# Weight blocks with their columns from the last to the first, streamed with a step of minus one

## The chip, the cores and the metric

The kernel runs on one core of one Trainium2 chip. The metric is the device time of one execution in microseconds, as the median of several runs. A hardware profile of one execution goes with it.

## What is computed

One decoder layer over 256 tokens of width 4096. The input is normed, multiplied with one wide weight, split into the operands of two token mixers, and each mixer's result is projected, gated, added, and projected once more:

```
h = rms_norm(x, norm_gains)
z = h @ w_in                       # gq gk gv gg gdec sq sk sv sg ga gb
o_a = rms_norm(gla_mix(gq, gk, gv, log_a(gdec)), gla_norm_gains)
y_a = (o_a * silu(gg)) @ w_gla_out
o_b = swa_sink_mix(sq, sk, sv, sinks)
y_b = (o_b * silu(sg)) @ w_swa_out
merged = sigmoid(ga + b_gates[0]) * y_a + sigmoid(gb + b_gates[1]) * y_b
out = rms_norm(x + merged @ w_out, final_norm_gain)
```

All of it is in float32.

## The kernel before

Nearly all of the work is in `gemm` (line 125). One call computes 512 columns of a product of all 256 tokens with one weight. The tokens are two tiles of 128; each has an accumulator of 128x512 numbers in PSUM. The depth of the product (4096, or 2048 for w_gla and w_swa) is cut into k tiles of 128, and two k tiles make a chunk.

For every chunk SyncE issues one load of 512 KB into a `raw` tile (line 148; four buffers). ScalarE casts it to float32r, a float32 with fewer mantissa bits, which gives `hi` (line 154; three buffers), and VectorE puts what is left, raw - hi, into `lo` (line 155; three buffers). Load and split carry a higher priority than the rest, so that they run ahead of the products (line 147). The left operand `lhs` has been split in the same way. `products` (lines 131 to 138) then issues, for one token tile and each of the chunk's k tiles, three products: left hi with hi, left hi with lo, left lo with hi. Of each, the token tile's 128x128 block is the stationary operand, and the 512 columns of hi or lo are the moving operand. A chunk thus feeds 2 k tiles x 3 products x 2 token tiles = 12 products.

The blocks of w_in come in the order of `BLOCKS`: query, key, value and gate of the linear attention, key and value of the window attention, then w_gla's eight blocks, the query and gate blocks of the window attention, and for each of eight blocks of the merge gate A, gate B and w_swa. The eight blocks of w_out stand last. In the last one, chunks near the end are kept in a tile `hold` until the second token tile's products use them (`trail`). The first block is preceded chunk by chunk by the load and split of the input (`first_inputs`).

Small products of the attentions and transposes, on float32 data, lie between the blocks. The low-rank decay (lines 208 to 216) has a weight `wdec` of its own, which is loaded and split apart from `gemm`; its product at line 215 has 32 columns of `wd` as the stationary operand and the 512 columns of one k tile of `hT` as the moving one.

On the host, `_tiles` (line 566) puts each weight into the order in which its chunks are loaded: [block, K group, partition, k tile, 512]. `wdec` does not go through it.

Of the kernel before, what the change touches and what calls it, by code (L numbers as in the profile page):

```python
# [28 lines left out]
STG = 3  # L29
NEG = -3.4028234663852886e38  # L30

# 512-column blocks of w_in, in the order in which the host lays them out.
BLOCKS = []
for _g in range(2):
    BLOCKS += [("gq", _g), ("gk", _g)]
# [11 lines left out]
def trunk_kernel(  # L47
# [18 lines left out]
    nc = tc.nc  # L66
# [18 lines left out]
    nc.gpsimd.memset(mhalf, -0.5)  # L85

    def rms_scale(o, ssum, n):
        """o = (ssum / n + eps) ** -0.5"""
        nc.vector.tensor_scalar(o, ssum, 1.0 / n, EPS, ALU.mult, ALU.add)
        nc.gpsimd.tensor_tensor(o, o, mhalf[:, : o.shape[1]], ALU.pow)  # L90

# [1 line left out]
    hT = big.tile([P, KT, 2, S], F32R, tag="hT", name="hT")  # L93

    xsb = big.tile([P, KT, S], F32, tag="oT", name="xsb")

    def first_inputs(gp, ssq):
        """Loads the input as the first block needs it; its squares add up in ssq."""

        def before(k0, n):  # L100
            with tc.high_priority(PRIO):
                if k0 < 4 or k0 % 4 == 0:
                    m = n if k0 < 4 else 4
                    nc.sync.dma_start(xsb[:, k0 : k0 + m, :], xT[:, k0 : k0 + m, :])
                for kt in range(k0, k0 + n):
                    g = gin_sb[:, kt : kt + 1]
                    nc.scalar.activation(hT[:, kt, 0, :], xsb[:, kt, :], AF.Copy, scale=g)
                    nc.vector.scalar_tensor_tensor(
                        hT[:, kt, 1, :], xsb[:, kt, :], g, hT[:, kt, 0, :].bitcast(F32), ALU.mult, ALU.subtract
                    )  # L110
            xr = xsb[:, k0 : k0 + n, :]
            if k0 < KW:
                nc.scalar.activation(ssq[:, k0 : k0 + n, :], xr, AF.Square)
                return
            sq = gp.tile([P, KW, S], F32, tag="sq", name=f"sq{k0}", bufs=2)
            nc.scalar.activation(sq, xr, AF.Square)
            nc.gpsimd.tensor_tensor(ssq, ssq, sq, ALU.add)

        return before
# [3 lines left out]
    RAMP = [(k, 1) for k in range(KW)] + WHOLE[1:]  # L123

    def gemm(name, lhs, w, nkt, before=None, chunks=WHOLE, trail=0, hold=None):
        """Both token tiles of lhs.T @ w for one block of 512 columns. The second tile's products
        with the last `trail` chunks come after all of the first tile's; those of these chunks
        that the staging area can't keep until then are in `hold`."""
        acc = [acc_ps.tile([P, NB], F32, tag="acc", name=f"{name}_a{t}") for t in range(NT)]

        def products(t, k0, n, hi, lo):
            ts = slice(t * P, (t + 1) * P)
            for i in range(n):
                kt = k0 + i
                lh, ll = lhs[:, kt, 0, ts], lhs[:, kt, 1, ts]
                nc.tensor.matmul(acc[t], lh, hi[:, i, :], start=kt == 0, stop=False)  # L136
                nc.tensor.matmul(acc[t], lh, lo[:, i, :], start=False, stop=False)  # L137
                nc.tensor.matmul(acc[t], ll, hi[:, i, :], start=False, stop=kt == nkt - 1)  # L138

        chunks = [c for c in chunks if c[0] < nkt]  # L140
        held = []
        for ci, (k0, n) in enumerate(chunks):
            left = len(chunks) - ci
            if before is not None:
                before(k0, n)
            with tc.high_priority(PRIO):
                raw = stage.tile([P, n, NB], F32, tag="raw", name=f"{name}_r{k0}", bufs=4)
                nc.sync.dma_start(raw, w[k0 // KW][:, k0 % KW : k0 % KW + n, :])
                if STG < left <= trail:
                    hi, lo = hold[:, trail - left, 0], hold[:, trail - left, 1]  # L150
                else:
                    hi = stage.tile([P, n, NB], F32R, tag="hi", name=f"{name}_h{k0}")
                    lo = stage.tile([P, n, NB], F32R, tag="lo", name=f"{name}_l{k0}")
                nc.scalar.copy(hi, raw)  # L154
                nc.vector.tensor_tensor(lo, raw, hi.bitcast(F32), ALU.subtract)  # L155
            products(0, k0, n, hi, lo)
            if left <= trail:
                held.append((k0, n, hi, lo))
            else:
                products(1, k0, n, hi, lo)  # L160
        for h in held:
            products(1, *h)
        return acc
# [5 lines left out]
        return rstd[:, t : t + 1]  # L169

    def split_to(dst, src_ps):
        """dst[:, ..hi/lo.., :] from a PSUM tile of the same layout less the hi/lo axis."""
        hi, lo = dst
        nc.scalar.copy(hi, src_ps)
        nc.vector.tensor_tensor(lo, src_ps, hi.bitcast(F32), ALU.subtract)

    def transpose_split(oT, kt0, src, nk, name):
        """src [tokens, t, nk*128] -> oT[:, kt0:kt0+nk, hi/lo, tokens]"""
        for k2 in range(0, nk, 2):
            tp = pst(f"{name}_t{k2}")  # L180
            for k in range(2):
                for t in range(NT):
                    c = (k2 + k) * P
                    nc.tensor.transpose(
                        tp[:, k * S + t * P : k * S + (t + 1) * P], src[:, t, c : c + P], ident
                    )
            v = tp.rearrange("p (k s) -> p k s", k=2)
            ks = slice(kt0 + k2, kt0 + k2 + 2)
            split_to((oT[:, ks, 0, :], oT[:, ks, 1, :]), v)

    # ================= gated linear attention =================
    with tc.tile_pool(name="gla", bufs=1) as gp:
        ssq = gp.tile([P, KW, S], F32, name="ssq")
        q0 = zblock("gq", 0, before=first_inputs(gp, ssq), chunks=RAMP)
        k0 = zblock("gk", 0)
        oaT = big.tile([P, OKT, 2, S], F32R, tag="oT", name="oaT")

        # per-token scale of the input norm
        xps = pst("xps")
        for t in range(NT):  # L200
            for i in range(KW):
# [2 lines left out]
                )  # L204
        rms_scale(rstd, xps[:, 0:NT], DM)

        # low-rank decay input, transposed: rows 0-15 from w's high part, 16-31 from its low part
        wd_raw = stage.tile([P, KT, RANK], F32, tag="raw", name="wd_raw", bufs=4)
        nc.sync.dma_start(wd_raw, wdec)
        wd = gp.tile([P, KT, 2, RANK], F32R, name="wd")  # L210
# [26 lines left out]
        nc.gpsimd.memset(cmask.rearrange("p (n c) -> p n c", c=CH)[:, :, 0:1], 0.0)  # L237

        def headsT(name, acc, scale):
            """[tokens, 4 heads x 128] in PSUM -> [128, head, token]"""  # L240
            zt = gp.tile([P, NT, NB], F32, tag="zt", name=f"{name}_z")
            for t in range(NT):
                nc.scalar.activation(zt[:, t, :], acc[t], AF.Copy, scale=rs(t))
            o = gp.tile([P, 4, S], F32, tag=name[:2], name=f"{name}T")
            for j2 in range(2):
                tp = pst(f"{name}_tp{j2}")
                for j in range(2):
                    for t in range(NT):
                        c = (j2 * 2 + j) * P
                        nc.tensor.transpose(  # L250
                            tp[:, j * S + t * P : j * S + (t + 1) * P], zt[:, t, c : c + P], ident
                        )
                nc.vector.tensor_scalar(
                    o[:, 2 * j2 : 2 * j2 + 2, :].rearrange("p h s -> p (h s)"), tp, scale, None, ALU.mult
                )
            return o
# [4 lines left out]
        for g in range(2):  # L261
            accq = q0 if g == 0 else zblock("gq", g)
            qT = headsT(f"gq{g}", accq, DK**-0.5)

            # log decays of the group's heads and their running sums in each chunk
            l = gp.tile([P, 4, S], F32, tag="e0", name=f"l{g}")
            for j2 in range(2):
                lp = pst(f"lp{g}{j2}")
# [10 lines left out]
            a = gp.tile([P, 4, S], F32, tag="e1", name=f"a{g}")  # L279
# [34 lines left out]
            )  # L314
            nc.scalar.activation(d, d, AF.Exp)
            nc.vector.tensor_tensor(kT, kT, d, ALU.mult)
            # keys of chunks 0 and 1 as chunks 2 and 3 see them
            k2 = gp.tile([P, 4, 2 * CH], F32, tag="k2", name=f"k2{g}")
            k3 = gp.tile([P, 4, 2 * CH], F32, tag="k3", name=f"k3{g}")
            nc.vector.tensor_tensor(  # L320
# [5 lines left out]
            for p in range(2):  # L326
                pi = 2 * g + p
                accv = zblock("gv", pi)
                v = gp.tile([P, NT, 2 * DV], F32, tag="v", name=f"v{pi}")
                for t in range(NT):  # L330
                    nc.scalar.activation(v[:, t, :], accv[t], AF.Copy, scale=rs(t))

                # o = A @ v, a head at a time; A is kept transposed, [key, query]
                accg = None
                oraw = gp.tile([P, 2, NT, DV], F32, tag="oraw", name=f"oraw{pi}")
                ss = gp.tile([P, 2 * NT], F32, tag="ss", name=f"ss{pi}")
# [51 lines left out]
                        nc.vector.tensor_tensor(gt4[:, t, j, :], ov, gt4[:, t, j, :], ALU.mult)  # L388
                transpose_split(oaT, pi * 4, gt, 4, f"oa{pi}")

    # ================= sliding-window attention =================
    late = ctx.enter_context(tc.tile_pool(name="late", bufs=1))
    ya = late.tile([P, NT, DM], F32, tag="ya", name="ya")
    with tc.tile_pool(name="swa", bufs=1) as sp:
# [100 lines left out]
                nc.vector.tensor_tensor(on[:, t, :], on[:, t, :], sg, ALU.mult)  # L495
            transpose_split(obT, i * 4, on, 4, f"ob{i}")

    # ================= gates and merge =================
    def merged(n):
        transpose_split(mT, n * 4, ya[:, :, n * NB : (n + 1) * NB], 4, f"m{n}")  # L500

# [21 lines left out]
                nc.vector.tensor_tensor(sig[1][:, t, :], acc[t], sig[1][:, t, :], ALU.mult)  # L523
                nc.vector.tensor_tensor(ya[:, t, cs], ya[:, t, cs], sig[1][:, t, :], ALU.add)

    # ================= output projection, residual, final norm =================
    with tc.tile_pool(name="fin", bufs=1) as fp:
        gf = fp.tile([P, DM], F32, name="gf")
        nc.scalar.dma_start(gf, gfin.partition_broadcast(P))
        hold = None  # L530
# [33 lines left out]


def _tiles(w, nblk):
    """[K, nblk*512] -> [block, K group, partition, k tile, 512], contiguous for each load."""
    import numpy as np

    k = w.shape[0]  # L570
    w = w.reshape(k // (KW * P), KW, P, nblk, NB)
    return np.ascontiguousarray(w.transpose(3, 0, 2, 1, 4))


# [53 lines left out]
```

## Time and profile before

| | us |
|---|---|
| median of 3 runs | 2496.63 |
| lowest and highest | 2496.22, 2498.13 |
| span of the profiled execution, first to last instruction | 2494.7 |
| TensorE shows matmuls | 2469.9 |
| TensorE shows weight loads (beside the matmuls) | 2033.3 |
| VectorE busy | 1306.1 |
| ScalarE busy | 1093.1 |
| GpSimd busy | 41.4 |
| HBM read and written | 468.23 MB, 4.19 MB |

In a row of the profile PE is TensorE's matmul, PEld its load of a stationary operand, DVE is VectorE, ACT ScalarE, POOL GpSimd and SP SyncE; SPq is SyncE's queue. L136 is line 136 of the kernel. A matmul is shown from its start to a modelled end, and the following ones start before that end, so its duration is longer than its place in the stream. A product on float32 operands shows as two records, one on float32r operands as one.

### The profile page before, as it was taken

How to read it: one execution, taken by the hardware profiler on the slowest of the kernel's cores; microseconds unless marked ns; L12 is line 12 of the kernel's file. 1: busy time of each engine (PE TensorE's matmuls, PEld its weight loads, DVE VectorE, ACT ScalarE, POOL GpSimd, SP SyncE). 2: the span in 40 equal slices, each digit the busy share in tenths (PEclk: the TensorE clock that was granted, in tenths of full speed). 3: DMA queues.
4: the chain of work that ended last, by engine and by line, in shares of the span. 5: the costliest groups of instructions: out<-in, count | busy, mean ns of one | idle time of the engine just before them, and what ended most of it. 6: DMA issues, size and time to landing. Idle time of an engine off the chain costs nothing.

```text
span 2494.7 us, 28744 instructions
## 1 busy us (share of the span) xinstructions
PE 2469.9 (99%) x11220; PEld 2033.3 (82%) x11220; DVE 1306.1 (52%) x1303; ACT 1093.1 (44%) x1289; POOL 41.4 (2%) x52
## 2 busy tenths in 40 slices
PE   8999999999999999999999999999999999999998
PEld 6788888888888888888888888888888888888886
DVE  8565555545444455555555454555545456544544
ACT  6444444434444444544444444444444444444443
POOL 4000000000000000000000000000000000000000
PEclk9999999999999999999999999999999999999999
DMA  7455555445555545454465556665666555665655
GB/s 258 156 175 188 170 175 195 175 168 188 194 192 195 193 148 193 150 171 166 150 211 199 198 198 197 197 202 197 198 196 198 194 194 177 236 211 203 211 203 186
DMA packets 132985, 474.32 MB, mean 190 GB/s; under 512 B 15056, under 2 KB 15440, under 8 KB 132720
## 3 DMA queue, kind: packets, MB, share of 16 engines
q1 hardware_dynamic: 127584, 461.69, 54.5%
q10 hardware_dynamic: 5264, 10.79, 1.4%
q8 instruction: 88, 1.44, 0.2%
q14 instruction: 49, 0.40, 0.0%
HBM read 468.23 MB, written 4.19 MB: 189 GB/s over the span
## 4 chain that ended last, share of the span: by engine, by line
PE 95%; DVE 2%; issue 1%; ACT 1%; DMA 0%; POOL 0%; SPq 0%; ACTq 0%; POOLq 0%; DVEq 0%
PE ga_a L137 5%; PE ga_a L136 5%; PE gb_a L137 5%; PE gb_a L136 5%; PE ga_a L138 5%; PE gb_a L138 5%; PE o_a L136 5%; PE o_a L137 5%; PE o_a L138 5%; PE sg_a L137 2%; PE sg_a L136 2%; PE sg_a L138 2%; PE sq_a L138 2%; PE sq_a L137 2%; PE ya_a L136 2%; PE ya_a L137 2%
## 5 line engine op out<-in xcount | busy, mean ns | idle before, releaser
L155 DVE TENSOR_TENSOR ga_l<-ga_r,ga_h 128x1024 fp32r<-128x1024 f32 x128 | 156.8, 1225 | 171.6 <-ACT ga_h L154 171.6
L155 DVE TENSOR_TENSOR gb_l<-gb_r,gb_h 128x1024 fp32r<-128x1024 f32 x128 | 156.9, 1225 | 171.1 <-ACT gb_h L154 171.1
L155 DVE TENSOR_TENSOR o_l<-o_r,o_h 128x1024 fp32r<-128x1024 f32 x124 | 152.0, 1225 | 161.4 <-ACT o_h L154 161.3
L154 ACT CAST ga_h<-ga_r 128x1024 fp32r<-128x1024 f32 x128 | 135.2, 1057 | 209.8 <-PE ga_a L138 171.5
L154 ACT CAST gb_h<-gb_r 128x1024 fp32r<-128x1024 f32 x128 | 135.2, 1056 | 204.5 <-PE gb_a L138 159.4
L154 ACT CAST o_h<-o_r 128x1024 fp32r<-128x1024 f32 x124 | 131.0, 1056 | 193.2 <-PE o_a L138 186.2
L138 PE MATMUL ga_a<-ga_h,hT 128*128 128x512 f32 x512 | 199.4, 389 | 0.0
L137 PE MATMUL ga_a<-ga_l,hT 128*128 128x512 f32 x512 | 199.2, 389 | 0.0
L136 PE MATMUL ga_a<-ga_h,hT 128*128 128x512 f32 x512 | 199.2, 389 | 0.0
L138 PE MATMUL gb_a<-gb_h,hT 128*128 128x512 f32 x512 | 199.2, 389 | 0.0
L136 PE MATMUL gb_a<-gb_h,hT 128*128 128x512 f32 x512 | 199.2, 389 | 0.0
L137 PE MATMUL gb_a<-gb_l,hT 128*128 128x512 f32 x512 | 199.2, 389 | 0.0
L138 PE MATMUL o_a<-o_h,mT 128*128 128x512 f32 x496 | 193.0, 389 | 0.0
L137 PE MATMUL o_a<-o_l,mT 128*128 128x512 f32 x496 | 193.0, 389 | 0.0
L136 PE MATMUL o_a<-o_h,mT 128*128 128x512 f32 x496 | 192.9, 389 | 0.0
L155 DVE TENSOR_TENSOR ya_l<-ya_r,ya_h 128x1024 fp32r<-128x1024 f32 x64 | 78.4, 1226 | 95.6 <-ACT ya_h L154 95.6
L155 DVE TENSOR_TENSOR sq_l<-sq_r,sq_h 128x1024 fp32r<-128x1024 f32 x64 | 78.4, 1225 | 84.8 <-ACT sq_h L154 84.8
L155 DVE TENSOR_TENSOR yb_l<-yb_r,yb_h 128x1024 fp32r<-128x1024 f32 x64 | 78.4, 1225 | 82.8 <-ACT yb_h L154 82.8
L155 DVE TENSOR_TENSOR gg_l<-gg_r,gg_h 128x1024 fp32r<-128x1024 f32 x64 | 78.3, 1224 | 75.9 <-ACT gg_h L154 75.9
L155 DVE TENSOR_TENSOR sg_l<-sg_r,sg_h 128x1024 fp32r<-128x1024 f32 x64 | 78.3, 1223 | 72.7 <-ACT sg_h L154 72.7
L154 ACT CAST sg_h<-sg_r 128x1024 fp32r<-128x1024 f32 x64 | 67.4, 1053 | 111.0 <-PE sg_a L138 94.7
L155 DVE TENSOR_TENSOR gv_l<-gv_r,gv_h 128x1024 fp32r<-128x1024 f32 x64 | 78.2, 1224 | 67.9 <-ACT gv_h L154 67.9
(278 smaller groups left out, 5568.3 us busy)
## 6 DMA issues: line engine op xcount, KB each, us to landing
ga_r<-in_win_dram SPq DMA_DIRECT2D x128, 512.0 KB, 4.3
gb_r<-in_win_dram SPq DMA_DIRECT2D x128, 512.0 KB, 4.2
o_r<-in_wout_dram SPq DMA_DIRECT2D x128, 512.0 KB, 3.3
gv_r<-in_win_dram SPq DMA_DIRECT2D x64, 512.0 KB, 3.2
gg_r<-in_win_dram SPq DMA_DIRECT2D x64, 512.0 KB, 3.3
ya_r<-in_wgla_dram SPq DMA_DIRECT2D x64, 512.0 KB, 3.2
sq_r<-in_win_dram SPq DMA_DIRECT2D x64, 512.0 KB, 3.2
sg_r<-in_win_dram SPq DMA_DIRECT2D x64, 512.0 KB, 3.3
```

The lines of the kernel that those rows point to most:

```text
L136: nc.tensor.matmul(acc[t], lh, hi[:, i, :], start=kt == 0, stop=False)
L137: nc.tensor.matmul(acc[t], lh, lo[:, i, :], start=False, stop=False)
L138: nc.tensor.matmul(acc[t], ll, hi[:, i, :], start=False, stop=kt == nkt - 1)
L154: nc.scalar.copy(hi, raw)
L155: nc.vector.tensor_tensor(lo, raw, hi.bitcast(F32), ALU.subtract)
```

## The change

The columns of each block of 512 are laid out in reverse on the host, and the products read them in reverse:

```diff
--- before.py
+++ after.py
@@ -133,9 +133,9 @@
             for i in range(n):
                 kt = k0 + i
                 lh, ll = lhs[:, kt, 0, ts], lhs[:, kt, 1, ts]
-                nc.tensor.matmul(acc[t], lh, hi[:, i, :], start=kt == 0, stop=False)
-                nc.tensor.matmul(acc[t], lh, lo[:, i, :], start=False, stop=False)
-                nc.tensor.matmul(acc[t], ll, hi[:, i, :], start=False, stop=kt == nkt - 1)
+                nc.tensor.matmul(acc[t], lh, hi[:, i, ::-1], start=kt == 0, stop=False)
+                nc.tensor.matmul(acc[t], lh, lo[:, i, ::-1], start=False, stop=False)
+                nc.tensor.matmul(acc[t], ll, hi[:, i, ::-1], start=False, stop=kt == nkt - 1)
...
@@ -564,12 +564,12 @@
 def _tiles(w, nblk):
...
     k = w.shape[0]
     w = w.reshape(k // (KW * P), KW, P, nblk, NB)
-    return np.ascontiguousarray(w.transpose(3, 0, 2, 1, 4))
+    return np.ascontiguousarray(w[..., ::-1].transpose(3, 0, 2, 1, 4))
```

The four weights w_in, w_gla, w_swa and w_out all go through `_tiles`, and all their products through these three lines. The two reversals cancel, so column j of an accumulator is column j of the block as before. What the diff changes beside this are comments.

## Rows read from the trace of the kernel before

**Rows 1.** The page's head: the span, and each engine's busy time, share and instructions.
```profile
span 2494.7 us, 28744 instructions
PE 2469.9 (99%) x11220; PEld 2033.3 (82%) x11220; DVE 1306.1 (52%) x1303; ACT 1093.1 (44%) x1289; POOL 41.4 (2%) x52
```

**Rows 2.** The page's 40 slices: busy tenths, DMA share in tenths, GB/s.
```profile
PE   8999999999999999999999999999999999999998
...
DMA  7455555445555545454465556665666555665655
GB/s 258 156 175 188 170 175 195 175 168 188 194 192 195 193 148 193 150 171 166 150 211 199 198 198 197 197 202 197 198 196 198 194 194 177 236 211 203 211 203 186
```

**Rows 3.** Stretches, TensorE alone: length, busy (records), granted clock, DMA share, GB/s.
```profile
core 0: us, PE busy (x), PEclk, DMA share, GB/s
0.00:60.00 60.00, 49.07 (x199) 1.00 0.75 262
60.00:2480.00 2420.00, 2416.82 (x11006) 1.00 0.56 188
```

**Rows 4.** The chain that ended last: shares of the span by engine.
```profile
PE 95%; DVE 2%; issue 1%; ACT 1%; DMA 0%; POOL 0%; SPq 0%; ACTq 0%; POOLq 0%; DVEq 0%
```

**Rows 5.** Costliest groups: out<-in, shapes, count, busy us, mean ns, idle before, releaser.
```profile
L155 DVE TENSOR_TENSOR ga_l<-ga_r,ga_h 128x1024 fp32r<-128x1024 f32 x128 | 156.8, 1225 | 171.6 <-ACT ga_h L154 171.6
...
L154 ACT CAST ga_h<-ga_r 128x1024 fp32r<-128x1024 f32 x128 | 135.2, 1057 | 209.8 <-PE ga_a L138 171.5
...
L137 PE MATMUL ga_a<-ga_l,hT 128*128 128x512 f32 x512 | 199.2, 389 | 0.0
L136 PE MATMUL ga_a<-ga_h,hT 128*128 128x512 f32 x512 | 199.2, 389 | 0.0
```

**Rows 6.** Timeline, TensorE, a quiet stretch: start us, length us, instruction; 19 products.
```profile
1899.81 0.39 PE L136 MATMUL yb_a<-yb_h,obT 128*128 128x512 f32 x1
1900.03 0.39 PE L137 MATMUL yb_a<-yb_l,obT 128*128 128x512 f32 x1
1900.26 0.39 PE L138 MATMUL yb_a<-yb_h,obT 128*128 128x512 f32 x1
...
1903.89 0.39 PE L136 MATMUL yb_a<-yb_h,obT 128*128 128x512 f32 x1
```

**Rows 7.** Instructions of a tile: shortest/median/longest ns, first and last start us.
```profile
L136 PEld LDWEIGHTS ga_a<-ga_h,hT x512: 187/188/192, 1256.6 to 2062.1; 128*128 128x128 f32 x171
```

**Rows 8.** The same view of line 215, the low-rank product.
```profile
L215 PEld LDWEIGHTS dps<-hT,wd x32: 107/108/113, 102.8 to 109.8; 128*32 128x32 f32 x32
L215 PE MATMUL dps<-hT,wd x32: 387/392/400, 102.9 to 110.0; 128*32 128x512 f32 x32
```

**Rows 9.** DMA issues: count, KB each, median us from issue to landing.
```profile
ga_r<-in_win_dram SPq DMA_DIRECT2D x128, 512.0 KB, 4.3
```

**Rows 10.** Waits: ScalarE's longest on TensorE, and all of TensorE's; us, times, longest.
```profile
ACT ga_h L154 <- PE ga_a L138: 171.5, 104, 1.7
...
PE gq_a L136 <- ACT gq_h L154: 5.7, 2, 5.4
PE gq_a L137 <- DVE gq_l L155: 5.2, 6, 1.9
PE op L365 <- POOL ats L359: 2.4, 4, 0.6
PE gv_a L137 <- DVE gv_l L155: 0.5, 1, 0.5
PE gk_a L137 <- DVE gk_l L155: 0.3, 1, 0.3
```

**Rows 11.** Timeline, TensorE, products on float32 operands, two records each.
```profile
163.24 0.59 PE L366 MATMUL op<-v,ats 128*128 128x256 f32 x2
163.68 0.59 PE L367 MATMUL op<-v,ats 128*128 128x256 f32 x2
164.11 0.33 PE L345 MATMUL at<-qs,ks 128*128 128x64 f32 x2
```

**Rows 12.** Timeline, TensorE, a block's start: the first and last of nine products.
```profile
115.20 0.39 PE L138 MATMUL gv_a<-gv_h,hT 128*128 128x512 f32 x1
...
117.04 0.39 PE L137 MATMUL gv_a<-gv_l,hT 128*128 128x512 f32 x1
```

## The prediction

> **What bounds the kernel now.** I read the page's head first [rows 1]: TensorE shows work in 2469.9 of 2494.7 us, VectorE in 1306.1, ScalarE in 1093.1. A matmul's end is modelled in this profile, so a busy share near 99% alone doesn't prove that TensorE is the limit. The 40 slices come next [rows 2]: TensorE is at nine tenths in all but the first and the last, and the DMA engines are mostly half to two thirds busy. From 60 to 2480 us the granted clock is 1.00, its upper level of 2.4 GHz [rows 3]. The chain of work that ended last then settles it [rows 4]: 95% of the span is TensorE's own, and no other engine has more than 2%.
>
> What sets TensorE's own time is read from the distance between starts, not from durations. A product of the weight stream (128x512, lines 136 to 138) is shown as 389 ns long [rows 5], but the next one starts long before that. In the timeline of a quiet stretch 19 products start between 1899.81 and 1903.89 us [rows 6]: 4.08 us over 18 steps is 226.7 ns each. There are 38 blocks of w_in with 32 k tiles, 8 blocks each of w_gla and w_swa with 16, and 8 blocks of w_out with 32, each k tile with 3 products for 2 token tiles: (38x32 + 16x16 + 8x32) x 6 = 10368 products, of the 11220 matmul records of [rows 1]. 10368 x 226.7 ns = 2350 us, or 94% of the span, which agrees with the chain. So every nanosecond on the distance of these products is worth 10.4 us, or 0.42%. That is the number on which the whole case hangs.
>
> Does the moving stream (the 512 columns of hi or lo) set the 226.7 ns, or the load of the stationary tile in front of each product? A load takes 188 ns [rows 7], and it starts beside the product before it. The low-rank product (line 215) streams 512 columns of the same type against a stationary tile of only 32 columns: its loads take 108 ns, yet 32 of them start from 102.9 to 110.0 us [rows 8], 7.1/31 = 229 ns apart. A shorter load doesn't bring the products closer, so the load isn't the limit. At 2.4 GHz one column a cycle makes 512/2.4 = 213.3 ns; 13.3 ns of the 226.7 are something else, and no row tells whether the stream itself needs them.
>
> **The change, part by part.**
> The layout: each block's 512 columns are reversed on the host, ahead of the launch. The shape, the bytes and the order of chunks in memory are as before, so a load stays 512 KB from the same places, with 4.3 us to landing [rows 9]; nothing is added to SyncE's queue, and no DMA is moved past another. Cost 0.
> The split: the cast (1057 ns) and the subtraction (1225 ns) run over 128x1024 numbers whose order has no meaning for them [rows 5]. Cost 0. Even a change here would lie in cover: a chunk feeds 12 products, 12 x 226.7 = 2720 ns, and ScalarE waits for TensorE to give a staging buffer back rather than the other way [rows 10].
> The tiles that aren't reversed: the decay weights (lines 208 to 212) aren't laid out by the function that reverses, and their product at line 215 isn't touched. `hold`, in the last block, is filled from reversed chunks and read by the same three lines, so it fits. The results leave each product in the old order, and everything behind the accumulators is as before. Cost 0.
> The products: the moving operand now starts at column 511 and goes down by 4 bytes at a time. Instructions, their count, stationary tiles, outputs and waits are the same. The only unknown of the case is whether TensorE reads a descending row as fast as an ascending one. No row shows a step of minus one on any engine, so I bound it from both sides. Below: at best the 13.3 ns above the 512 columns go away, 10368 x 13.3 = 138 us. Above: the fp32 products at lines 366 and 367 take their moving columns at a lower rate, under the same full clock. Two records of 256 columns start 163.24, two more 163.68, the next group 164.11 us [rows 11], so a record takes 0.87/4 = 217 ns, 0.85 ns a column against 0.44. A descending read at that rate would make 435 ns a product, 10368 x (435 - 226.7) = +2160 us. Between these far ends I take 0: the nearest rows by far are the same products themselves, with the same type, the same number of bytes from the same row of the same tile, read in four-byte steps.
> The page "SBUF — State Buffer" of the Trainium skill, in the section Door 1: The DMA port swizzle (its note on cachelines), bears on this: on-chip memory is read in lines of 16 bytes, accesses that stay in a line run at full rate, and at least two of them are needed to cover a new line. By that rule a descending fp32 row still has four accesses a line, and its cost would be nothing; no run here shows it yet.
>
> The sum: 0 on a profiled span of 2494.7 us. The median of the three times, 2496.6 us (2496.2 to 2498.1), lies 1.9 us above that span; this doesn't change. Forecast 2496.6 us.
>
> **How closely 0 is known.** The same products don't keep one distance everywhere. From 115.20 to 117.04 us eight steps take 230.0 ns each [rows 12], 3.3 ns more than in [rows 6], with the same form and clock. I take this 3.3 ns as the smallest shift that the kernel shows by itself, 10368 x 3.3 = 34 us or 1.4%, and put it on either side.
>
> **The rivals.**
> Half rate (the other side): the reader of the moving operand fetches ahead upwards and serves a descending row column by column or pair by pair at the rate of [rows 11]. Its place is each of the 10368 products, its price +2160 us, less at most the 11 us that the first blocks' products wait for their casts anyway [rows 10], so about 4650 us. It decides as soon as the stream needs more than the 226.7 ns that a product has, that is, below 512/226.7 = 2.26 columns a nanosecond. For it: the stream runs close to one column a cycle and so has almost nothing to give away. Against it: nothing in the trace.
> A start cost: the rate stays, but a product that begins at the end of a row pays a few cycles. At 3.3 ns a product this gives 2531 us, at 13.3 ns 2635 us. For it: TensorE has no gap in the middle of the span, so nothing would cover it. Against it: the 13.3 ns may themselves be slack in which it disappears.
> Here the page "TensorE: Matmul & The Clock Gate" of the Trainium skill, in Back-to-back issue gap, gives N/2.4 + 2.5 ns, 215.8 ns for 512 columns. The row is 226.7 ns, and the measurement decides; if the page's figure is what the stream alone needs, 11 ns of a start cost would be free.
> Faster: the 13.3 ns have to do with the order in which a row is read (the stationary tile and the columns come from the same memory), and descending reads lose fewer of them. The bound is 2496.6 - 138 = 2358 us, with 3.3 ns 2462 us. Against it: the distance of line 215, whose tiles lie elsewhere and load faster, is no shorter [rows 8]. The loads could follow: a chunk every 2560 ns is 205 GB/s, and the first slice moved 258 [rows 2].
> The change does something else than it says: the order of the instructions shifts, because the writer of the waits sees a reversed row as another region. A wait that then ends late would show at the first product of a chunk; for one block that is a few microseconds, of which TensorE shows 0.8 us in all behind the first block now [rows 10]. Its time is within some 10 us of the forecast.
>
> **How the numbers follow.** No change in the distance 0.68, the start cost 0.10, half rate or worse 0.14, faster 0.06, something else 0.02 (put half to same, half to slower). Faster or slower by 0.2% is 5 us, or half a nanosecond a product; a measurement of this kernel tells no less. So slower 0.25, same 0.69, faster 0.06. For the range I take the shift of 3.3 ns below, 2462 us, and the start cost up to 13.3 ns above, 2635 us; it leaves out half rate and the larger gain, together about 0.17. The likeliest case's own range is 2490 to 2503 us.
>
> **What would show it.** If I am right, the 128x512 products keep 389 ns and start 226.7 ns apart, their loads keep 188 ns, and the casts wait as long for TensorE as before. With a start cost the distance grows by some nanoseconds, alike in all blocks, while line 215, which isn't reversed, keeps its 229 ns; that line is the control in either trace. With half rate it is near 435 ns, the DMA share falls to about a third, and the waits of ScalarE for TensorE grow by some 2.5 us a chunk. Wrong altogether would be a shift in the time that doesn't show in the distance of the products: then instructions were reordered, and the waits of TensorE name the line.

## The result: 2.5% slower

The reversed kernel takes 2558.9 us (2558.8 to 2559.0) against 2496.6 us, a ratio of 1.0248 with a 95% interval of 1.023 to 1.0267. Its profiled span is 2557.3 us, 62.6 us longer.

The page's head, the stretches of TensorE alone and the chain by engine of the kernel after, with the columns of [rows 1], [rows 3] and [rows 4]:

```profile
span 2557.3 us, 28744 instructions
...
PE 2534.0 (99%) x11220; PEld 2036.4 (80%) x11220; DVE 1306.0 (51%) x1303; ACT 1085.7 (42%) x1289; POOL 41.2 (2%) x52
```
```profile
0.00:60.00 60.00, 49.72 (x198) 1.00 0.76 261
60.00:2480.00 2420.00, 2417.69 (x10740) 1.00 0.56 184
```
```profile
PE 97%; DVE 1%; issue 1%; DMA 0%; ACT 0%; POOL 0%; SPq 0%; ACTq 0%; POOLq 0%
```

The instructions are as many as before, the granted clock is the same 1.00, and TensorE still is the chain. But in the stretch from 60 to 2480 us 10740 matmul records lie where 11006 lay in [rows 3]. The groups, the loads of one tile, the instructions of line 215 and a gap-free stretch of the timeline, as in [rows 5], [rows 7], [rows 8] and [rows 6]:

```profile
L155 DVE TENSOR_TENSOR ga_l<-ga_r,ga_h 128x1024 fp32r<-128x1024 f32 x128 | 156.9, 1226 | 181.6 <-ACT ga_h L154 181.6
...
L154 ACT CAST ga_h<-ga_r 128x1024 fp32r<-128x1024 f32 x128 | 133.9, 1046 | 221.2 <-PE ga_a L138 180.8
...
L137 PE MATMUL ga_a<-ga_l,hT 128*128 128x512 f32 x512 | 203.5, 397 | 0.0
```
```profile
L136 PEld LDWEIGHTS ga_a<-ga_h,hT x512: 188/188/192, 1283.7 to 2112.7; 128*128 128x128 f32 x171
```
```profile
L215 PEld LDWEIGHTS dps<-hT,wd x32: 107/108/113, 104.3 to 111.2; 128*32 128x32 f32 x32
L215 PE MATMUL dps<-hT,wd x32: 387/392/397, 104.3 to 111.5; 128*32 128x512 f32 x32
```
```profile
1297.88 0.40 PE L138 MATMUL ga_a<-ga_h,hT 128*128 128x512 f32 x1
...
1306.29 0.40 PE L138 MATMUL ga_a<-ga_h,hT 128*128 128x512 f32 x1
```

The reversed products are shown as 397 ns instead of 389, and between the two timeline rows lie 36 steps: 8.40 us / 36 = 233.3 ns against 226.7 (the starts are in the trace to a nanosecond; the timeline prints them to ten, so its rows are 8.41 us apart). The product at line 215, which isn't reversed, keeps its 392 ns and its distance: with starts to a nanosecond it is 230.2 ns before and 230.1 after, where the prediction had 229 from rounded rows. The loads stay at 188 ns, the subtraction at 1226 ns, and ScalarE only waits a little longer for TensorE (180.8 us for 171.5 of [rows 10]). Over the whole trace, the steps from one block product straight to the next (those under 340 ns) sum up to 2332.7 us before (10247 steps) and 2397.6 us after (10246): 64.9 us more, 6.4 ns a step. That is the whole loss; 2 us came back between the blocks and in the opening.

From here on the distance of a kind of product is the time from the first start to the last of a gap-free stretch, divided by its steps.

### The profile page after: what moved, and what is told of

Same layout as the page of the kernel before. It is cut to its first block, busy times and chain, and to the rows that moved or that the text cites. A ratio compares the mean times of both kernels' runs of the same rounds, so it can differ in the third digit from the quotient of the medians.

```text
span 2557.3 us, 28744 instructions
## 1 busy us (share of the span) xinstructions
PE 2534.0 (99%) x11220; PEld 2036.4 (80%) x11220; DVE 1306.0 (51%) x1303; ACT 1085.7 (42%) x1289; POOL 41.2 (2%) x52
## 4 chain that ended last, share of the span: by engine, by line
PE 97%; DVE 1%; issue 1%; DMA 0%; ACT 0%; POOL 0%; SPq 0%; ACTq 0%; POOLq 0%
PE ga_a L137 5%; PE gb_a L137 5%; PE gb_a L138 5%; PE ga_a L138 5%; PE ga_a L136 5%; PE gb_a L136 5%; PE o_a L137 5%; PE o_a L136 5%; PE o_a L138 5%; PE sg_a L137 2%; PE sg_a L136 2%; PE gv_a L137 2%; PE ya_a L136 2%; PE sg_a L138 2%; PE sq_a L137 2%; PE sq_a L138 2%
## 5 line engine op out<-in xcount | busy, mean ns | idle before, releaser
L155 DVE TENSOR_TENSOR ga_l<-ga_r,ga_h 128x1024 fp32r<-128x1024 f32 x128 | 156.9, 1226 | 181.6 <-ACT ga_h L154 181.6
L155 DVE TENSOR_TENSOR gb_l<-gb_r,gb_h 128x1024 fp32r<-128x1024 f32 x128 | 156.9, 1226 | 181.3 <-ACT gb_h L154 181.3
L154 ACT CAST ga_h<-ga_r 128x1024 fp32r<-128x1024 f32 x128 | 133.9, 1046 | 221.2 <-PE ga_a L138 180.8
L138 PE MATMUL ga_a<-ga_h,hT 128*128 128x512 f32 x512 | 203.6, 398 | 0.0
L136 PE MATMUL gb_a<-gb_h,hT 128*128 128x512 f32 x512 | 203.5, 397 | 0.0
L138 PE MATMUL gb_a<-gb_h,hT 128*128 128x512 f32 x512 | 203.5, 397 | 0.0
L136 PE MATMUL ga_a<-ga_h,hT 128*128 128x512 f32 x512 | 203.5, 397 | 0.0
L138 PE MATMUL o_a<-o_h,mT 128*128 128x512 f32 x496 | 197.1, 397 | 0.0
L136 PE MATMUL o_a<-o_h,mT 128*128 128x512 f32 x496 | 197.0, 398 | 0.0
L155 DVE TENSOR_TENSOR yb_l<-yb_r,yb_h 128x1024 fp32r<-128x1024 f32 x64 | 78.5, 1226 | 87.8 <-ACT yb_h L154 87.7
```

The source lines that it names most:

```text
L136: nc.tensor.matmul(acc[t], lh, hi[:, i, ::-1], start=kt == 0, stop=False)
L138: nc.tensor.matmul(acc[t], ll, hi[:, i, ::-1], start=False, stop=kt == nkt - 1)
```

## The experiments

The theory after the result was that a descending stream pays a fixed 6.7 ns, as a start cost. The rivals were a slightly lower rate, and the place of the first column. Since every kind of block shows its own distance, one kernel can hold many variants: a read order by kind, with the stored order of the columns changed to match.

**Which part of the order costs (e1).**

```diff
+PATS = {"ga": "rev", "gb": "lines_down", "o": "in_line_down", "yb": "halves_down", "ya": "in_half_down", "sq": "pairs_down", "sg": "in_pair_down", "gv": "step2", "gg": "step2_down"}
...
+    if pat == "in_line_down":
+        return ap.rearrange("p (a b) -> p a b", b=4)[:, :, ::-1]
...
+    if pat == "lines_down":
+        return ap.rearrange("p (a b) -> p a b", b=4)[:, ::-1, :]
...
+    if pat == "rev":
+        return ap[:, ::-1]
+    if pat == "step2":
+        return ap.rearrange("p (b a) -> p a b", a=2)
...
-                nc.tensor.matmul(acc[t], lh, hi[:, i, :], start=kt == 0, stop=False)
...
+                nc.tensor.matmul(acc[t], lh, view(hi[:, i, :], pat), start=kt == 0, stop=False)
```

> Same result as the kernel before; the stored order and the read order are changed together, with another order for each kind of block: ga all 512 down; gb 128 groups of four, groups down, columns in a group up; o groups of four up, columns in a group down; yb halves down, columns in a half up; ya halves up, columns in a half down; sq pairs down, up in a pair; sg pairs up, down in a pair; gv even columns, then odd ones; gg odd columns down, then even ones down; gq, gk, sk, sv as before. Read by the distance of starts in each kind. Theory A, a fixed cost of a product whose innermost step is negative (what the two traces show: 226.7 to 233.3 ns): ga, o, ya, sg, gg 233 ns, gb, yb, sq, gv 227. Theory B, the reader's rate falls slightly whenever it goes back to a lower address: gb like ga (128 steps back), yb hardly anything (one step back), o and sg like ga or worse. Theory C, the cost is in where the stream starts (the last column of the row, not the first of a group): ga, gg 233, and o 233, since its first column is the fourth of a group, sg too; gb 227 (starts at the first column of a group), ya 233.

Timeline, TensorE, first and last start of 36 steps, in ga, gb, o and gv:

```profile
1634.71 0.40 PE L200 MATMUL ga_a<-ga_h,hT 128*128 128x512 f32 x1
...
1643.11 0.40 PE L200 MATMUL ga_a<-ga_h,hT 128*128 128x512 f32 x1
...
1673.44 0.40 PE L198 MATMUL gb_a<-gb_h,hT 128*128 128x512 f32 x1
...
1681.84 0.40 PE L198 MATMUL gb_a<-gb_h,hT 128*128 128x512 f32 x1
...
2537.74 0.39 PE L198 MATMUL o_a<-o_h,mT 128*128 128x512 f32 x1
...
2545.90 0.39 PE L198 MATMUL o_a<-o_h,mT 128*128 128x512 f32 x1
...
131.55 0.63 PE L199 MATMUL gv_a<-gv_l,hT 128*128 128x512 f32 x1
...
147.79 0.63 PE L199 MATMUL gv_a<-gv_l,hT 128*128 128x512 f32 x1
```

| order | ns |
|---|---|
| all 512 down (ga) | 233.3 |
| groups of four down, inside a group up (gb); pairs down (sq) | 233.3, 233.3 |
| groups of four up, inside a group down (o); inside a pair down (sg) | 226.7, 226.7 |
| halves down, inside a half up (yb); inside a half down (ya) | 226.7, 233.3 |
| step of two, up (gv), down (gg) | 451.1, 466.7 |

All three theories fail here. gb's innermost step is up and it pays; o's is down and it doesn't (against A). o begins at the last column of a group for nothing, gb at the first and pays (against C). o goes down at three steps of four for nothing (against B as it was put). At the places of this kernel, what counts is the order in which the groups of four columns, 16 bytes, are visited; the order within a group is free.

**The same for the whole kernel, timed (e8).** The edit is o's order for every block.

```diff
+PATS = {"ga": "in_line_down", "gb": "in_line_down", "o": "in_line_down", "yb": "in_line_down", "ya": "in_line_down", "sq": "in_line_down", "sg": "in_line_down", "gv": "in_line_down", "gg": "in_line_down", "gq": "in_line_down", "gk": "in_line_down", "sk": "in_line_down", "sv": "in_line_down"}
...
+    if pat == "in_line_down":
+        return ap.rearrange("p (a b) -> p a b", b=4)[:, :, ::-1]
```

> Same result. In every block, each group of four columns (16 bytes) is reversed in place and read back to front, the groups themselves in ascending order: 511 of 512 steps inside the stream are as irregular as in the reversed kernel, three of four go down. If descending steps as such cost, 2560 us or more. If only the order of the 16-byte groups counts, 2496 us, no difference from the kernel before.

2496.8 us, ratio 1.000 (0.999 to 1.001). Negative steps as such cost nothing here.

**Columns and the width of the stationary operand (e3).**

```diff
+                m, cols, down = SPEC.get(name.rstrip("0123456789"), (P, NB, 0))
+                if kt in (0, nkt - 1):
+                    m, cols, down = P, NB, 0
...
+                o_ = acc[t][0:m, 0:cols]
+                nc.tensor.matmul(o_, lh[:, 0:m], mv(hi), start=kt == 0, stop=False)
```

> Leaves work out: in all k tiles but a block's first and last, some kinds of blocks use only 32 columns of the stationary operand or fewer columns of the moving one. ga 32 stationary columns, 384 moving, up; gb the same, down; ya and yb 32 and 256, up and down; gv and gg 32 and 512, up and down; sq and sg 128 and 448, up and down; o 128 and 512, down, on an unturned layout. Theory A (a fixed cost a product): down minus up is 6.7 ns at 512, 448, 384 and 256 alike, and up is columns/2.4 plus 13.3 ns: 200 at 448, 173 at 384, 120 at 256 (unless the loads of 108 ns set it there). Theory B (a rate, 1.3% of the columns): down minus up is 6.7 at 512, 5.8 at 448, 5.0 at 384, 3.3 at 256.

Up and down: 231.7 and 233.3 ns at 512 columns with 32 stationary columns, 173.4 and 175.5 at 384, 117.8 and 117.8 at 256 (for a while 113.3 up); 202.7 and 206.7 at 448 with all 128. Down minus up is 6.6 ns at 512 with 128 stationary columns ([rows 6] and this kernel's o), but 1.7 with 32. So it is neither a fixed cost nor a share of the columns, and with fewer stationary columns an ascending product got slower. These are the two rows, 36 steps apart, of the ascending one with 32:

```profile
122.22 0.39 PE L149 MATMUL gv_a<-gv_l,hT 128*32 128x512 f32 x1
...
130.56 0.39 PE L149 MATMUL gv_a<-gv_l,hT 128*32 128x512 f32 x1
```

The 202.7 ns hold in three of the four ascending blocks with 448 columns. The second, sq1, settles at 206.7 behind an interruption by small products, though form, direction and place are the same. Its first two rows below are 36 steps apart, and so are the two of sq3:

```profile
920.20 0.37 PE L150 MATMUL sq_a<-sq_h,hT 128*128 128x448 f32 x1
...
927.64 0.37 PE L150 MATMUL sq_a<-sq_h,hT 128*128 128x448 f32 x1
...
1086.04 0.37 PE L150 MATMUL sq_a<-sq_h,hT 128*128 128x448 f32 x1
...
1093.34 0.36 PE L150 MATMUL sq_a<-sq_h,hT 128*128 128x448 f32 x1
```

So one place can have more than one steady distance. Which one a stream falls into wasn't tested; sq2 and sq3 are interrupted as well and come back to 202.7.

**Place of the stream (e2, e4, e5).**

```diff
-                    hi = stage.tile([P, n, NB], F32R, tag="hi", name=f"{name}_h{k0}")
...
+                    hi = stage.tile([P, n * NB + 4], F32R, tag="hi", name=f"{name}_h{k0}")
...
+                    hi = hi[:, off : off + n * NB].rearrange("p (n c) -> p n c", n=n)
```

> Same result as the kernel before. hi and lo lie in tiles with 4 more columns, so that a block's columns can start 1 or 3 columns later. ga: up, 1 column later; sg: up, 3 columns later; gb: down, 1 column later (the first column read is then the first of a group of four); sq: down, in place; o: hi down, lo up (the subtraction writes lo turned); yb: hi up, lo down; gv: step of four, up; the rest up, in place. Theory A (a fixed cost of each descending product): ga, sg 227, gb, sq 233; in o the steps of lines 136 and 138 are 6.7 ns longer and the mean of three is 231; in yb only line 137's step, mean 229. Theory C (place of the first column): ga and sg 233 though they ascend, gb 227 though it descends. Theory D (a change of direction between neighbouring products costs, not the direction): o and yb at least 233 in the mean, with the longer step on whichever follows a turn.

The kinds that should have been the control spoke first: the blocks of w_gla, all up and in place, went from 226.7 to 231.7 ns. With 16 bytes more, each tile takes 32 bytes more of memory, so the buffers no longer begin at the same place within 2048 bytes. The others lie between 229.0 and 236.1 with no order by direction: up one column later 236.1, up three later 229.0, down one later 235.6, down in place 233.7. The turn of lo alone (o 233.6, yb 232.0) can't be told from that, so theory D stayed open here; but in the reversed kernel no product turns, and it pays. With 16 columns more instead of 4 (e4 up, e5 down):

> Same result as the kernel before, all products up. Each hi and lo tile has 16 columns more, so the three buffers of each begin 64 bytes apart from a multiple of 2048, and by kind the columns start later in them: gq, gk, sk, sv, gg 0 columns, sq 1, ya 2, gv 3, ga 4, sg 6, gb 8, yb 12, o 16. The run before showed that 16 bytes more per tile raise an ascending product from 226.7 to 231.7 ns, so the distance is not a fixed sum of the product alone. If the place within 16 bytes is what costs: sq, ya, gv, sg above 230, the others 226.7. If the place within 64 bytes is: ga, gb, yb above 230 as well, gg and o 226.7. If the distance between the stream's address and that of the stationary operand, whose load runs beside it, is what costs, all kinds change, those at 0 columns too, and the distance differs from buffer to buffer with a period of three chunks.

> Same result; the places of the run before, with all products down and the turned layout. If a descending stream costs 6.7 ns by itself, every kind is 6.7 ns above its ascending place. If descending only makes another pattern of meetings with the load beside it, the difference changes with the place and is smaller, or below zero, where the ascending product is at 231 ns or more; every kind then lies near 233 to 236.

No kind of e4 stays at 226.7: behind the opening block the means by kind go from 230.0 to 236.9. Within a kind the distances repeat after 36 products, which is three chunks or one turn of the buffers. Descending adds 2.1 ns at 0 columns, 0.4 at 8, 3.0 at 2, 9.4 at 3, and takes 0.9 away at 1. A price of its own would have been the same everywhere.

**The other operand (e6).**

```diff
+        oaT = big.tile([P, OKT * 2 * S + 32], F32R, tag="oT", name="oaT")
+        oaT = oaT[:, LATER["oaT"] : LATER["oaT"] + OKT * 2 * S].rearrange("p (k w s) -> p k w s", k=OKT, w=2)
...
+                if kind in ST_ONE:
+                    lh, ll = lh[:, 0:1].broadcast_to([P, P]), ll[:, 0:1].broadcast_to([P, P])
+                if kind in ST_STEP2:
+                    lh, ll = lhs[:, kt, 0, t::2], lhs[:, kt, 1, t::2]
```

> Changes part of the computation: ga and gb use one column of the stationary operand 128 times, sg and gg every second column over both token tiles, and gb, sq and gg read the moving columns down on an unturned layout. ya, yb and o (all up) read a stationary operand that begins 4, 16 and 32 columns later. All moving tiles are in their old places. If the cost belongs to the descending stream alone: ga, sg, ya, yb, o 226.7, gb, sq, gg 233.3. If it comes from the load of the next stationary operand, which walks through the same memory beside the stream: ga and gb are alike, since that load then stays at one address, and away from 226.7 and 233.3; ya, yb, o leave 226.7; sg and gg shift.

The places are not those that were meant. The wider tiles made the places of hT and of oT 128 bytes longer each, and the staging tiles lie behind them. So all streams begin 256 bytes later, and against its stationary operand the stream lies 112 bytes later in ya, 64 in yb, 128 in o, and 256 in the kinds that read hT. The 256 bytes do no harm: gq, gk, gv, sk and sv, which are otherwise as before, keep 226.7 ns.

Timeline, 36 steps each, of gv, of ga (one stationary column 128 times, ascending), of yb and of o:

```profile
226.34 0.39 PE L153 MATMUL gv_a<-gv_h,hT 128*128 128x512 f32 x1
...
234.50 0.39 PE L153 MATMUL gv_a<-gv_h,hT 128*128 128x512 f32 x1
...
1282.59 0.40 PE L155 MATMUL ga_a<-ga_h,hT 128*128 128x512 f32 x1
...
1290.91 0.40 PE L155 MATMUL ga_a<-ga_h,hT 128*128 128x512 f32 x1
...
1365.70 0.39 PE L153 MATMUL yb_a<-yb_h,obT 128*128 128x512 f32 x1
...
1373.94 0.39 PE L153 MATMUL yb_a<-yb_h,obT 128*128 128x512 f32 x1
...
2184.45 0.39 PE L153 MATMUL o_a<-o_h,mT 128*128 128x512 f32 x1
...
2192.81 0.39 PE L153 MATMUL o_a<-o_h,mT 128*128 128x512 f32 x1
```

With the stream as in gv (8.16/36 = 226.7 ns), one stationary column 128 times makes an ascending product 231.1 ns (8.32/36), and every second column (sg) 233.3. The stationary operand is read by nothing but the load, which runs beside the product before, so what the load reads changes the distance of products whose stream is untouched. Descending streams show 233.3 with each of the three stationary patterns (gb, gg, sq). That ga and gb would be alike was wrong: 231.1 and 233.3.

yb takes 8.24/36 = 228.9 ns, o 8.36/36 = 232.2, and ya stays at 226.7. The scan that follows, at the same places against each other (64, 128 and 112 bytes), has 228.9, 233.3 and 231.1.

**A scan (e7), and the two operands' places changed alone and together (e9 to e11).** In e7 the buffers all begin where they did within 512 bytes, and the block number moves the columns; to make room, three small tiles of the attentions have one buffer instead of two (in e12 too). In e9 to e11 the only edit is an unused tile of 32 bytes, set to zero once: ahead of the staging tiles in the kernel before (e9) and in the reversed one (e10), ahead of both operands in the kernel before (e11).

```diff
+LATER = {'ga': (0, 4), 'gb': (32, 4), 'o': (64, 4), 'ya': (96, 4), 'yb': (0, 1), 'sq': (8, 8), 'sg': (40, 8), 'gv': (72, 8), 'gg': (104, 8)}
...
+                    hi = stage.tile([P, n * NB + 128], F32R, tag="hi", name=f"{name}_h{k0}")
...
+                    hi = hi[:, off : off + n * NB].rearrange("p (n c) -> p n c", n=n)
```
```diff
+    gap = ctx.enter_context(tc.tile_pool(name="gap", bufs=1))
+    nc.gpsimd.memset(gap.tile([P, 8], F32, name="gap8"), 0.0)
     stage = ctx.enter_context(tc.tile_pool(name="stage", bufs=STG))
```

> Same result as the kernel before. hi and lo have 128 columns (512 bytes) more, so that all buffers begin at the same place within 512 bytes as before, and the block number decides how much later the columns start: ga, gb, o, ya (up) 0 to 124 columns in steps of 4 (16 bytes), yb (up) 0 to 7 columns in steps of 1; sq, sg, gv, gg (down, turned layout) 8 to 128 columns in steps of 8; gq, gk, sk, sv (up) 0. If the distance of products depends on the direction alone: up 226.7 and down 233.3 throughout. If it depends on how the stream and the load beside it lie to each other: up 226.7 at a shift of 0 (and, by the run with a shifted stationary operand, near 16 bytes), 228 to 234 at most other shifts, and down with its own best shifts, some perhaps below 233.3. A shift that gives less than 226.7 would make a faster kernel.

| columns later, up | 0 | 4 | 8 | 12 | 16 | 20 | 24 | 28 |
|---|---|---|---|---|---|---|---|---|
| ns (ga) | 226.7 | 231.7 | 233.3 | 233.3 | 228.9 | 231.1 | 233.3 | 231.1 |
| and 32 more (gb) | 233.3 | 233.3 | 234.3 | 233.3 | 233.3 | 234.6 | 233.3 | 236.7 |

From 64 columns (256 bytes) on, o repeats ga's row; its last block falls from 231.1 to 226.7 where it reads from `hold`, which isn't moved. ya at 96 to 124 repeats gb's row but in two places: 231.1 at 108 and 226.7 at 124, for which I have no reason. One to seven columns later (yb) gives 227.8 to 237.2. Descending: 233.3 to 233.5 in 15 of 16 places, 236.7 in one.

> The kernel before with one change: 32 unused bytes per partition between the tiles of the left operands and the staging tiles, so that every hi and lo begins 32 bytes later against the stationary operand. All products go up. If the distance of products depends on how the two lie to each other (the scan gave 233.3 ns at 8 columns): 10368 x 6.6 ns = 63 to 69 us more, about 2560 us, what the reversed kernel takes. If direction alone counts: 2496 us.

> The reversed kernel with the same 32 bytes. If descending has a price of its own on top of the place: 2497 + 2 x 62, about 2620 us. If descending and a shifted place are two ways to lose the same thing (the scan gave 233.3 ns for descending streams at nearly all places): 2559 us, no difference from the reversed kernel.

> The kernel before with the 32 bytes ahead of both the left operands and the staging tiles, so that both begin 32 bytes later and lie to each other as before. If only the place against each other counts: 2496 us and 226.7 ns. If the place in memory as such counts: 2560 us.

| kernel | us | ratio to before, interval | ns a product in ga |
|---|---|---|---|
| e9: up, stream 32 bytes later | 2558.8 | 1.0249, 1.0232 to 1.0266 | 233.3 |
| e10: down, stream 32 bytes later | 2558.5 | 1.0246, 1.0231 to 1.0261 | 233.3 |
| e11: up, both 32 bytes later | 2496.5 | 1.000, 0.9991 to 1.001 | 226.7 |

Timelines of e9 and of e11, 36 steps each:

```profile
1296.77 0.39 PE L140 MATMUL ga_a<-ga_h,hT 128*128 128x512 f32 x1
...
1305.17 0.39 PE L140 MATMUL ga_a<-ga_h,hT 128*128 128x512 f32 x1
```
```profile
1272.67 0.39 PE L140 MATMUL ga_a<-ga_h,hT 128*128 128x512 f32 x1
...
1280.83 0.39 PE L140 MATMUL ga_a<-ga_h,hT 128*128 128x512 f32 x1
```

e9 is the kernel before with no column reversed, and it loses the same 62 us: 8.40/36 = 233.3 ns. In e10 the reversed kernel loses nothing more from the same shift. In e11 the streams lie in the same place in memory as in e9, and only the left operands have moved, so that the two lie to each other as before; the loss is gone.

**Two places at once (e12).** hi and lo are moved apart, 56 pairs of places, to look for a kernel faster than both.

```diff
+                    hi = hi[:, off : off + n * NB].rearrange("p (n c) -> p n c", n=n)
+                    lo = lo[:, off_lo : off_lo + n * NB].rearrange("p (n c) -> p n c", n=n)
```

> Same result as the kernel before, all products up, in the scan's tiles. hi and lo are moved apart: hi starts 0 (ga), 4 (gb), 8 (o), 16 (ya), 32 (yb), 48 (sq, sg) or 60 columns later (gv, gg), lo 0, 4, 8, 16, 24, 32, 48 or 60 columns by the block's number. If each product loses by its own place against the load beside it, the distances are means of the scan's values (two thirds hi's, one third lo's), and no pair is below the 226.7 ns of 0 and 0. If two places can make up for each other, some pair is below; that pair would make a kernel faster than the one before.

0 and 0 gives 226.7 ns, one other pair (hi 48, lo 4 columns later) the same, the others 228.8 to 235.0. None is below. The values are no means of the scan's: with hi at 48 and lo in place it is 234.4. So no faster version was found. Nor does a place repeat its value in every run: with both 60 columns later gg has 233.3 ns here, and gb had 236.7 in the scan; with both 32 later yb has 232.2, and gb had 233.3.

## Why the prediction was wrong

**The term that was 0.** The sum had one open term, 10368 products times the cost of a descending read, and I put it at 0. It measured 6.4 ns a step, 64.9 us. The bounds (13.3 ns below, 208 above) held it, and 2558.9 us lies where I had put the start cost, not in the likeliest case's 2490 to 2503. The other terms came out as put: layout and split cost nothing on the path, the tiles that aren't reversed kept their durations.

**The step that failed first.** "A shorter load doesn't bring the products closer, so the load isn't the limit" took the duration of the load as its only way to matter. The runs show that what counts is where the load reads while the stream reads. Other columns for the load alone make an ascending product 231.1 or 233.3 ns instead of 226.7 (e6). Under streams that lie in the same place, moving the left operands by 32 bytes takes it from 233.3 to 226.7 (e9 and e11). The trace of before had the sign in it. The product at line 215 had a shorter load and yet 229 ns [rows 8] (230.2 by starts to a nanosecond), and the products of the blocks took 230.0 ns at a block's start [rows 12]. I read the one as proof that the load is harmless and the other as scatter; both streamed 512 columns of the same type at another distance, which a stream with a fixed cost of its own can't show.

**The argument for 0.** "The nearest rows by far are the same products themselves" held for form, bytes and row, but not for the order in which 16-byte groups are visited against the load. The note on cachelines of the Trainium skill's page "SBUF — State Buffer" (section Door 1: The DMA port swizzle) had four accesses to a 16-byte line at full rate, so a cost of nothing. e1 and e8 agree that the order inside 16 bytes is free. The rest they don't bear out: visiting the groups downwards costs 6.7 ns at the places of this kernel, and a step of two columns, with two accesses a line, takes 451 ns instead of 227. The measurements decide.

**The rivals.** Half rate is out (435 ns forecast, 233 measured). The start cost had sign, place and size, but not the mechanism: a cost at the end of a row would not shrink to 1.7 ns with 32 stationary columns, nor appear in a kernel without a reversed column (e9). That the reader "fetches ahead upwards" isn't needed to explain anything either. Faster was not found: no order and no place tried went below 226.7 ns with 512 columns and 128 stationary ones. That the instructions are reordered is out as well: the same instructions stand in the same order on every engine, and the whole difference lies in the distance of the products.

**What is shown and what isn't.** Shown: the distance depends on how the moving and the stationary operand lie to each other, though that alone doesn't fix it (sq in e3, and the same places in e6, e7 and e12); the kernel before stands at the best place found, with both operands at the same place within 512 bytes; going down and moving by 32 bytes each lose 6.7 ns there, and not twice. Argued only: that load and stream hinder each other at the memory's read side. What exactly meets there, why one place can have two steady distances, why descending is 233.3 ns at nearly all places of the scan but up to 239.4 in e5, and what the 13.3 ns of the best case are, stays open. A stationary operand read in the other direction, which would test it from the other side, wasn't tried.

## What to carry to other kernels

Where one kind of matmul is 94% of the time, its distance from start to start is the number to know, and a few nanoseconds on it are per cents. This distance isn't a property of the shape: compare the same form in several places of the trace, and if it differs, look at how the two operands lie to each other before calling it scatter. When a harmless edit (a pad, a small new tile, another order of allocation) costs 2%, check whether it moved one operand of the matmuls against the other, and pad the other one too.

## What the runs showed of the hardware that was not expected

- 32 unused bytes between the two operands' tiles cost 62 us (2496.2 to 2558.8 us); the same 32 bytes ahead of both cost nothing (2496.5 us).
- A float32r stream with a step of two columns takes 451 ns for 512 columns, twice the 227 ns of a step of one; going down in it costs another 15.6 ns.
- Reversing the columns inside each 16 bytes is free (226.7 ns, 2496.8 us); reversing the order of the 16-byte groups is not (233.3 ns), at the places of this kernel.
- With 32 stationary columns instead of 128, an ascending product of 512 columns is slower, 231.7 ns against 226.7.
- The same form in the same direction at the same place settled at 202.7 ns in three blocks of e3 and at 206.7 in a fourth.
- The distances repeat to a nanosecond: 233, 226, 234 ns over and over in ga of e6, and a period of 36 products, one turn of the three buffers, in e2 and e4.
